# Router logits from the plain residual, filler products on TensorE, pinned places for scatter, gather and transposes, and expert products in steps of four

## The chip, the core and the metric

The kernel runs on one core of a Trainium2 chip. The metric is the device time of one launch in microseconds (us); the profile is one execution of it taken apart by the hardware profiler. Five engines matter: TensorE (PE in the profile; PEld is its weight load), VectorE (DVE), ScalarE (ACT), GpSimd (POOL) and SyncE (SP), which issues nearly all transfers.

## The reference, cut to what matters

Two layers of a hybrid backbone over 256 latent and 256 context tokens of width 1024. The change lies in the second layer's feed-forward part, a mixture of eight SwiGLU experts of which each latent token takes two:

```python
x = x + mod_x[2] * (y_x @ w_out[i])
...
x = x + mod_x[5] * ffn(_modulate(_rms(x, norm2_w[i]), mod_x[3], mod_x[4]))
...
def _modulate(h, shift, scale):
    return h * (1.0 + scale) + shift
...
def _moe(h, router, wg, wu, wd):
    logits = (h @ router).astype(jnp.float32)
    top_v, top_i = lax.top_k(logits, TOP_K)
    gates = jax.nn.softmax(top_v, axis=-1)
    y = jnp.zeros_like(h)
    for e in range(N_EXPERTS):
        w_e = jnp.sum(jnp.where(top_i == e, gates, 0.0), axis=-1).astype(h.dtype)
        y = y + w_e[..., None] * _swiglu(h, wg[e], wu[e], wd[e])
    return y
```

An expert is 1024 x 3584 for gate and up and 3584 x 1024 for down, in float32. A final RMSNorm follows.

## The kernel before

Everything up to the second layer's attention is as in any transformer kernel and isn't touched. What is touched begins with the output projection `project(1, CTX, acc)` (L965), a generator that yields after each step: eight steps for its first three output tiles together, then one for each of five more. Each output tile is added to the residual `x[k]` (128 features x 512 tokens) by DVE at L789, and its square is added to `acc` (L251 to L255).

**Router, L998 to L1071.** PE sums the squares (L288), DVE makes the reciprocal root with twelve small instructions (L266 to L271, L290), and PE spreads it over all partitions (L297, `rbc`). Then eight steps follow: DVE scales `x[k]` (L1013), ACT adds the shift and gives the modulated `hf[k]` (L1014), PE multiplies with the router (L1016, `lg`). The residual is transposed into `xt` beside this (L1006), the modulated tokens into `ht` (L1028). ACT copies the logits (L1018), PE transposes them (L1021), DVE picks the two best experts (L1037 to L1056), PE counts ranks (L1058 to L1062, `rk`), and DVE gets each token's slot in its expert (`pos`) and the counts.

**prepare, L1079.** For an expert, DVE builds a one-hot matrix `oh` of tokens against 96 slots (L1083); PE gathers with it the modulated tokens from `ht` (L1090, `ga`, 16 products, 32 records); ACT copies them into `G` (L1093); PE transposes `oh` (L1096) for the way back.

**experts, L1128.** Eight blocks, one per expert, in an order by how full they are. The 96 slots are three groups of 32. Groups 0 and 1 are always computed; group 2 only when the expert has more than 64 tokens, by an `If` on a PE register (L1136). In a block there are four `up` passes (two halves of the width, gate and up; eight weight tiles each) and one `down` pass (14 tiles). A step of either takes two weight tiles through groups 0, 2, 1, so a block has 16 + 7 such `If`s; the first of each pass has an `Else` that writes zeros. Four products of one tile and group run side by side in four column strips of PE (L1152, L1177); each is two records. Between the passes PE transposes the hidden values (`turn`, L1197), and after `down` `scatter` (L1102) adds up the strips on ACT and DVE (L1107 to L1114) and returns a generator whose eight products (L1121, L1122) add the result to `xt`. In the text these are written behind the next block's gate pass, but the order on each engine is made by a planner that moves an instruction ahead of others when it holds it to be ready.

**Weights.** `Ahead` (L928) streams 46 tiles per block (32 of 896 KB, 14 of 1 MB) from SP into a ring of 16 buffers: tile j+16 is issued when the last product on tile j is done (`load.done`). The first 16 are issued before the router. The numbers of the later experts are read by SP, and all eight group flags by PE, from what the router computed (L1303 to L1305), ahead of the first product.

## Time and profile before

| | us |
|---|---|
| median of three runs | 1833.72 (1830.26 to 1839.75) |
| the profiled execution | 1831.45 |
| its span, first to last instruction | 1829.7 |
| PE / DVE / ACT / POOL busy | 1730.8 / 587.1 / 445.1 / 22.5 |
| read from HBM | 469.36 MB |

The span is read in stages. Up to about 895 us come the first layer and the second layer's attention and projection; from 895 to 924 us the router; from 924 to 1805 us the eight expert blocks; then 25 us of the last scatter, the norm and the store. An engine's busy time says little of whether it bounds; the rows that end its waits do.

### The profile page before, as it was taken

How to read it: one execution, taken by the hardware profiler on the slowest of the kernel's cores; microseconds unless marked ns; L12 is line 12 of the kernel's file. 1: busy time of each engine (PE TensorE's matmuls, PEld its weight loads, DVE VectorE, ACT ScalarE, POOL GpSimd, SP SyncE). 2: the span in 40 equal slices, each digit the busy share in tenths (PEclk: the TensorE clock that was granted, in tenths of full speed). 3: DMA queues.
4: the chain of work that ended last, by engine and by line, in shares of the span. 5: the costliest groups of instructions: out<-in, count | busy, mean ns of one | idle time of the engine just before them, and what ended most of it. 6: DMA issues, size and time to landing. Idle time of an engine off the chain costs nothing. (4 is left out here: it accounts for less than half of the span.)

```text
span 1829.7 us, 31142 instructions
## 1 busy us (share of the span) xinstructions
PE 1730.8 (95%) x13016; PEld 980.7 (54%) x13016; DVE 587.1 (32%) x1356; ACT 445.1 (24%) x852; POOL 22.5 (1%) x47
## 2 busy tenths in 40 slices
PE   6999999999999999999889999999999999999995
PEld 4866458888888898765733333332333323333231
DVE  6635565633333348465410200201011020200213
ACT  4543553432222225544301000100010000100001
POOL 1001000000000000000000000000000000000000
PEclk9999999999999999999989999999999999999997
DMA  7435541332323224454869999898999989999892
GB/s 313 150 119 184 182 161 58 98 98 93 103 92 101 95 81 127 149 195 153 345 243 419 418 419 395 336 389 322 395 418 418 414 335 409 418 418 406 335 419 110
DMA packets 84861, 472.70 MB, mean 258 GB/s; under 512 B 9424, under 2 KB 9808, under 8 KB 69088
## 3 DMA queue, kind: packets, MB, share of 16 engines
q1 hardware_dynamic: 84240, 469.36, 67.4%
q8 instruction: 118, 1.93, 0.4%
q0 software_dynamic: 176, 0.56, 0.1%
q10 hardware_dynamic: 288, 0.52, 0.1%
q14 instruction: 39, 0.32, 0.0%
HBM read 469.36 MB, written 1.05 MB: 257 GB/s over the span
## 5 line engine op out<-in xcount | busy, mean ns | idle before, releaser
L1152 PE MATMUL up<-rawe,G 128*32 128x448 f32 x5120 | 517.7, 551 | 14.0 <-PEq L1136 8.9
L1152 PEld LDWEIGHTS up<-rawe,G 128*32 128x32 f32 x5120 | 168.6, 111 | 337.0 <-issue 309.6
L331 PE MATMUL mm<-hh,wh 128*128 128x512 f32 (+1 forms) x856 | 305.5, 360 | 4.3 <-ACT hh L326 4.2
L332 PE MATMUL mm<-hl,wh 128*128 128x512 f32 (+1 forms) x856 | 304.5, 356 | 0.0
L333 PE MATMUL mm<-hh,wl 128*128 128x512 f32 (+1 forms) x856 | 303.4, 355 | 0.0
L1177 PE MATMUL y<-rawe,e 128*32 128x512 f32 x2240 | 251.2, 594 | 4.0 <-PEq L1136 3.2
L145 ACT ACTIVATE wh<-raw 128x1024 fp32r<-128x1024 f32 x120 | 127.3, 1061 | 326.3 <-PE mm L332 291.2
L146 DVE TENSOR_TENSOR wl<-raw,wh 128x1024 fp32r<-128x1024 f32 x120 | 146.7, 1224 | 174.0 <-ACT wh L145 171.5
L331 PEld LDWEIGHTS mm<-hh,wh 128*128 128x128 f32 x856 | 161.0, 189 | 31.4 <-ACT hh L326 5.5
L332 PEld LDWEIGHTS mm<-hl,wh 128*128 128x128 f32 x856 | 161.8, 189 | 27.3 <-issue 5.2
L333 PEld LDWEIGHTS mm<-hh,wl 128*128 128x128 f32 x856 | 161.7, 189 | 23.5 <-issue 1.6
L1217 DVE TENSOR_TENSOR hid<-sg,up 128x448 f32<-128x448 f32 x48 | 27.1, 617 | 422.8 <-PE up L1152 422.8
L1177 PEld LDWEIGHTS y<-rawe,e 128*32 128x32 f32 x2240 | 73.4, 109 | 158.8 <-issue 151.0
L1109 DVE TENSOR_TENSOR ye<-y,yc 32x512 f32<-32x512 f32 x48 | 32.7, 682 | 200.0 <-ACT yc L1107 199.3
L1198 ACT ACTIVATE e<-hT 128x384 f32<-128x384 f32 x48 | 23.6, 492 | 283.7 <-PE hT L1197 283.1
L1213 ACT ACTIVATE sg<-up 128x448 f32<-128x448 f32 x48 | 22.8, 546 | 218.4 <-PE up L1152 218.4
L331 PE MATMUL mm<-fh,wh 128*128 128x512 f32 (+1 forms) x209 | 74.5, 356 | 0.0
L332 PE MATMUL mm<-fl,wh 128*128 128x512 f32 (+1 forms) x209 | 74.3, 355 | 0.0
L333 PE MATMUL mm<-fh,wl 128*128 128x512 f32 (+1 forms) x209 | 74.3, 355 | 0.0
L210 PE MATMUL ada<-araw,cz 128*32 128x256 f32 x640 | 54.3, 390 | 11.5 <-DMA araw<-in_ada_dram 11.0
L1107 ACT ACTIVATE yc<-y 64x512 f32<-64x512 f32 x24 | 14.3, 596 | 205.0 <-PE y L1177 199.8
L333 PEld LDWEIGHTS mm<-fh,wl 128*128 128x128 f32 x209 | 39.5, 189 | 5.6
(280 smaller groups left out, 1370.8 us busy)
## 6 DMA issues: line engine op xcount, KB each, us to landing
rawe<-in_mg_dram SPq DMA_DIRECT2D x128, 896.0 KB, 10.1
rawe<-in_mu_dram SPq DMA_DIRECT2D x128, 896.0 KB, 11.5
rawe<-in_md_dram SPq DMA_DIRECT2D x112, 1024.0 KB, 14.7
raw<-in_ws_dram SPq DMA_DIRECT2D x120, 512.0 KB, 3.6
araw<-in_ada_dram SPq DMA_DIRECT2D x80, 512.0 KB, 4.4
a<-in_ada_dram SPq DMA_DIRECT2D x8, 1024.0 KB, 11.7
xall<-in_xT_dram SPq DMA_DIRECT2D x2, 1024.0 KB, 6.6
fn<-in_fn_dram POOLq DMA_DIRECT2D x1, 512.0 KB, 5.9
```

Of the source, the lines that this page charges most:

```text
L145: act.activation(h, raw, AF.Copy)
L146: dve.tensor_sub(l, raw, h)
L210: pe.matmul(o[32 * g:32 * g + 32, 0:256], cz[:, kt, 16 - 2 * row:48 - 2 * row], t[:, z:z + 256], start=(first and kt < 4), stop=(last and ...
L331: pe.matmul(out, wh, hh, start=first, stop=False)
L332: pe.matmul(out, wh, hl, start=False, stop=False)
L333: pe.matmul(out, wl, hh, start=False, stop=last)
L1109: dve.tensor_add(ye[32 * s:32 * s + 32, n * 512:(n + 1) * 512], y[s][32 * n:32 * n + 32, :], yc[32 * n:32 * n + 32, :])
L1152: pe.matmul(o[s][32 * c:32 * c + 32, 0:SC], g[:, k, 32 * s:32 * s + 32], w[k][:, c * SC:(c + 1) * SC], start=(k == 0), stop=(k == KT - 1), ...
L1177: pe.matmul(y[s][r:r + 32, :], e[s][:, 2 * i + par, :], w[i - lo][:, par * 1024 + n * 512:par * 1024 + (n + 1) * 512], start=(i == 0), sto ...
L1198: act.activation(e[s][:, 12 * st:12 * st + 12, :], pt[:, 0:384].rearrange("p (q c) -> p q c", c=32), AF.Copy)
L1213: act.activation(sg[s], o[:, 0:SC], AF.Silu)
L1217: dve.tensor_mul(hid[st, s], sg[s], o[:, 0:SC])
```

## The change

The router multiplies the plain residual: the modulation's scale is multiplied into the router's weights ahead of time (`wr`), the shift gives a constant `lc`, and the reciprocal root (`rms`) is multiplied into the transposed logits. Four of the eight logit products are written into the projection. `ht` now holds the plain residual, so one set of transposes is gone; `xt` is copied from it. The gather's one-hot carries `rms`, and scale and shift are applied as `G` leaves PSUM, in eight instructions on ACT and DVE instead of two on ACT. After the transposes PE runs 16 products with zeros, after the ranks 4. `tc.issue_after(ins)` keeps the instructions of its block behind `ins` on the engine of `ins`: the scatter, the gather with the next flag's load, and both transposes of a block are tied so to the last group-1 product of a named step. Steps of `up` take four tiles, of `down` 4, 2, 4 and 4. PE's flags are read one per block instead of all at the start. The zero fills of `yh`, `yl` and `oht` move from GpSimd to ACT.

```diff
+WARM = (16, 4)
+UPS, DOWNS = (0, 4, 8), (0, 4, 6, 10, 14)
...
-    step(p, HEAD)
     wr0 = P1.tile([128, KT, NE], F32, name="wr0")
     nc.gpsimd.dma_start(wr0, a["router"])
+    step(p, HEAD)
...
+    scale, shift = (RW.tile([128, KT], F32, name=n) for n in ("scale", "shift"))
+    dve.scalar_tensor_tensor(scale, mod(1, 4, 0), 1.0, n2[:, 1, :], op0=ALU.add, op1=ALU.mult)
+    dve.tensor_copy(shift, mod(1, 3, 0))
-    nc.gpsimd.tensor_copy(wr[:, :, 0:NE], wr0)
-    A = coef(1, 1)
+    dve.tensor_mul(wr[:, :, 0:NE], wr0, scale.unsqueeze(2).to_broadcast([128, KT, NE]))
+    o = ps("ax", name="lc")
+    for k in range(KT):
+        pe.matmul(o[:, 0:NE], shift[:, k:k + 1].to_broadcast([128, 128]), wr0[:, k, :], start=(k == 0), stop=(k == KT - 1))
+    lc = RW.tile([128, NE], F32, name="lc")
+    act.activation(lc, o[:, 0:NE], AF.Copy)
+    def logits(ks):
+        for k in ks:
+            g = 32 * (k % 4)
+            last = pe.matmul(lg[g:g + 32, 0:256], wr[:, k, :], x[k][:, 256:], start=(k < 4), stop=(k >= 4),
+                             tile_position=(0, g))
+        return last.ins
+    step(p, KT - HEAD + 2)
+    lg = ps("mm", name="lg")
+    logits(range(4))
     run(p)
...
-    S = Stats(acc[0])
-    S.sums(CTX, TOK)
-    for t in range(2):
-        for c in range(2):
-            s = slice(c * 512, (c + 1) * 512)
-            p = ps("ax", name="xT")
-            for q in range(4):
-                pe.transpose(p[:, q * 128:(q + 1) * 128], x[4 * c + q][:, 256 + t * 128:384 + t * 128], ident)
-            act.activation(xt[:, t, s], p, AF.Copy)
-    b = S.spread(CTX, TOK)
-    lg = ps("mm", name="lg")
-    for k in range(KT):
-        u = P1.tile([128, 256], F32, tag="u", name="u", bufs=UB)
-        dve.scalar_tensor_tensor(u, x[k][:, 256:], A[:, k, 0:1], b[:, 256:], op0=ALU.mult, op1=ALU.mult)
-        act.activation(hf[k], u, AF.Identity, bias=mod(1, 3, 0)[:, k:k + 1])
-        g = 32 * (k % 4)
-        pe.matmul(lg[g:g + 32, 0:256], wr[:, k, :], hf[k], start=(k < 4), stop=(k >= 4), tile_position=(0, g))
+    behind_lg = logits(range(4, KT))
     lgs = P1.tile([128, 256], F32, tag="u", name="lgs", bufs=UB)
-    behind_lg = act.activation(lgs, lg[:, 0:256], AF.Copy).ins
-    lg = ps("mm", name="lgT")
-    for t in range(2):
-        pe.transpose(lg[:, t * 128:(t + 1) * 128], lgs[:, t * 128:(t + 1) * 128], ident)
+    act.activation(lgs, lg[:, 0:256], AF.Copy)
+    rms = RS.tile([128, 2], F32, name="rms")
+    with tc.issue_after(behind_lg):
+        o = ps("ax", name="ss")
+        for t in range(2):
+            pe.matmul(o[:, t:t + 1], acc[0][:, CTX + t * 128:CTX + (t + 1) * 128], ones, start=True, stop=True)
+        v = P1.tile([128, 4], F32, tag="v4", name="v4", bufs=2)
+        dve.tensor_scalar(v[:, 0:2], o[:, 0:2], 1.0 / D, EPS, op0=ALU.mult, op1=ALU.add)
+        rsqrt(P1, v[:, 0:2], rms, "n2")
+        lg = ps("mm", name="lgT")
+        for t in range(2):
+            behind_lg = pe.transpose(lg[:, t * 128:(t + 1) * 128], lgs[:, t * 128:(t + 1) * 128], ident).ins
+    def idle(n):
+        o = ps("mm", name="idle")
+        for _ in range(n):
+            pe.matmul(o, zb[:, 0:128], zb, start=True, stop=True)
...
     with tc.issue_after(behind_lg):
         for t in range(2):
             for c in range(2):
-                p = ps("ax", name="tT")
+                s = slice(c * 512, (c + 1) * 512)
+                p = ps("ax", name="xT")
                 for q in range(4):
-                    pe.transpose(p[:, q * 128:(q + 1) * 128], hf[4 * c + q][:, t * 128:(t + 1) * 128], ident)
-                s = slice(c * 512, (c + 1) * 512)
+                    pe_last = pe.transpose(p[:, q * 128:(q + 1) * 128], x[4 * c + q][:, 256 + t * 128:384 + t * 128], ident)
                 behind_th = act.activation(ht[:, t, s], p, AF.Copy).ins
+                last = pe_last.ins
+        with tc.issue_after(last):
+            idle(WARM[0])
...
+    dve.tensor_mul(l0, l0, bc(rms))
+    dve.tensor_add(l0, l0, lc.unsqueeze(1).to_broadcast([128, 2, NE]))
...
-    pe.matmul(rk[:, 2 * NE:3 * NE], onesb, selb[:, 1, :], start=False, stop=True)
+    with tc.issue_after(pe.matmul(rk[:, 2 * NE:3 * NE], onesb, selb[:, 1, :], start=False, stop=True).ins):
+        idle(WARM[1])
...
-        oh = XP.tile([128, 2, SLOTS], F32, tag="oh", name="oh", bufs=1)
+        oh, ohr = (XP.tile([128, 2, SLOTS], F32, tag=n, name=n, bufs=1) for n in ("oh", "ohr"))
         for t in range(2):
-            behind_oh[0] = dve.tensor_scalar(oh[:, t, :], iota[:, 0:SLOTS], poscol(t), None, op0=ALU.is_equal).ins
+            behind_oh[0] = dve.tensor_scalar(ohr[:, t, :], iota[:, 0:SLOTS], poscol(t), rms[:, t:t + 1],
+                                             op0=ALU.is_equal, op1=ALU.mult).ins
         g = XP.tile([128, KT, SLOTS], F32, tag="G", name="G", bufs=2)
         for n in range(2):
             p = ps("ax", name="ga")
             for q in range(4):
                 k = 4 * n + q
                 for t in range(2):
-                    pe.matmul(p[:, q * SLOTS:(q + 1) * SLOTS], ht[:, t, k * 128:(k + 1) * 128], oh[:, t, :],
+                    pe.matmul(p[:, q * SLOTS:(q + 1) * SLOTS], ht[:, t, k * 128:(k + 1) * 128], ohr[:, t, :],
                               start=(t == 0), stop=(t == 1))
-            pv = p[:, 0:4 * SLOTS].rearrange("p (q c) -> p q c", q=4)
-            act.activation(g[:, 4 * n:4 * n + 4, :], pv, AF.Copy)
+            for q in range(4):
+                k, z = 4 * n + q, p[:, q * SLOTS:(q + 1) * SLOTS]
+                if q % 2:
+                    dve.tensor_scalar(g[:, k, :], z, scale[:, k:k + 1], shift[:, k:k + 1], op0=ALU.mult, op1=ALU.add)
+                else:
+                    act.activation(g[:, k, :], z, AF.Identity, scale=scale[:, k:k + 1], bias=shift[:, k:k + 1])
+        for t in range(2):
+            dve.tensor_scalar(oh[:, t, :], iota[:, 0:SLOTS], poscol(t), None, op0=ALU.is_equal)
         p = ps("ax", name="ohT")
         for t in range(2):
             pe.transpose(p[0:SLOTS, t * 128:(t + 1) * 128], oh[:, t, :], ident)
...
                 else:
-                    body(s)
+                    behind[0] = body(s).ins
...
-            for k0 in range(0, KT, 2):
+            for k0, k1 in zip(UPS, UPS[1:]):
                 def body(s):
-                    for k in (k0, k0 + 1):
+                    for k in range(k0, k1):
...
                         if s == GROUPS[-1]:
                             load.done(KT - 1 - k)
+                    return last
...
                 groups(b, body, zero, k0 == 0)
+                if k1 == KT:
+                    for s in GROUPS:
+                        consume(s, o[s])
                 yield
-            for s in GROUPS:
-                consume(s, o[s])
...
-        def down(b, y, e, lo, hi):
-            w = load.take(hi - lo)
-            for i0 in range(lo, hi, 2):
+        def down(b, y, e):
+            w = {}
+            for i0, i1 in zip(DOWNS, DOWNS[1:]):
+                for i, t in enumerate(load.take(i1 - i0)):
+                    w[i0 + i] = t
...
-                    for i in (i0, i0 + 1):
+                    for i in range(i0, i1):
...
                         if s == GROUPS[-1]:
-                            load.done(hi - 1 - i)
+                            load.done(i1 - 1 - i)
+                    return last
...
                 u = up(b, g, st, gate)
-                step(u, 2)
+                step(u)
                 if st:
-                    turn([hid[0, i] for i in range(3)], e, 0)
+                    with tc.issue_after(behind[0]):
+                        turn([hid[0, i] for i in range(3)], e, 0)
                 run(u)
                 u = up(b, g, st, product)
-                if not st and pending:
+                for _ in range(2):
+                    if not st and pending:
+                        with tc.issue_after(behind[0]):
+                            step(pending)
                     step(u)
-                    step(pending)
-                    step(u)
-                    step(pending)
                 run(u)
             y = [ps("y", name="y") for _ in range(3)]
-            u = down(b, y, e, 0, 6)
-            step(u, 2)
-            turn([hid[1, i] for i in range(3)], e, 1)
-            run(u)
-            u = down(b, y, e, 6, 14)
+            u = down(b, y, e)
+            step(u)
+            with tc.issue_after(behind[0]):
+                turn([hid[1, i] for i in range(3)], e, 1)
             step(u, 2)
             if b + 1 < len(blocks):
-                nxt = prepare(blocks[b + 1][0])
+                with tc.issue_after(behind[0]):
+                    nxt = prepare(blocks[b + 1][0])
+                    if flags:
+                        flags.append(flag(b + 1))
             run(u)
             pending = scatter(y, oht, blocks[b][1])
         run(pending)
...
     for z in (yh, yl, *(o.rearrange("p t c -> p (t c)") for o in ohts)):
-        nc.gpsimd.tensor_copy(z[SLOTS:128, :], zb[SLOTS:128, 0:1].to_broadcast([128 - SLOTS, z.shape[1]]))
+        with tc.issue_after(behind_th):
+            act.activation(z[SLOTS:128, :], zb[SLOTS:128, 0:1].to_broadcast([128 - SLOTS, z.shape[1]]), AF.Copy)
+    with tc.issue_after(behind_th):
+        for t in range(2):
+            act.activation(xt[:, t, :], ht[:, t, :], AF.Copy)
...
-    flags = [nc.values_load(f[0:1, p:p + 1], engines=(mybir.EngineType.PE,), min_val=0, max_val=1)
-             for p, f in enumerate([third0] + [third] * (NE - 1))]
-    experts(blocks, loader, first, flags)
+    def flag(p):
+        return nc.values_load((third if p else third0)[0:1, p:p + 1], engines=(mybir.EngineType.PE,), min_val=0, max_val=1)
+    experts(blocks, loader, first, flag)
```

## Rows read from the trace of the kernel before

**Rows 1.** Windows: stretch, length, busy (count) PE/PEld/DVE/ACT/POOL, PEclk, DMA share, GB/s.

```profile
924.20:1019.20 95.00, 89.61 (x810) 34.02 (x814) 5.93 (x15) 8.11 (x15) 0.00 (x0) 0.96 0.92 376
...
1019.20:1143.30 124.10, 121.66 (x1174) 42.90 (x1170) 15.23 (x27) 9.64 (x19) 0.00 (x0) 0.99 1.01 410
...
1489.40:1587.10 97.70, 90.95 (x826) 32.83 (x822) 15.19 (x27) 9.58 (x19) 0.00 (x0) 0.97 0.96 387
...
1711.20:1804.80 93.60, 86.83 (x792) 29.36 (x788) 14.42 (x24) 8.64 (x17) 0.00 (x0) 0.96 0.83 334
```

**Rows 2.** Waits, experts' stretch: who waited for whom, total us, times, longest.

```profile
PE up L1152 <- PEq L1136: 8.9, 38, 1.1
...
PE up L1152 <- DMA rawe<-in_md_dram: 0.2, 1, 0.2
```

**Rows 3.** Timeline of SP: start, us, queue, line, transfer, count.

```profile
878.17 20.67 SPq L943 DMA_DIRECT2D rawe<-in_mu_dram  x8
...
932.15 10.27 SPq L943 DMA_DIRECT2D rawe<-in_mg_dram  x8
```

**Rows 4.** Windows of 40 us within the first block.

```profile
960.00:1000.00 40.00, 38.76 (x364) 16.56 (x359) 4.16 (x12) 5.41 (x11) 0.00 (x0) 1.00 1.01 419
```

**Rows 5.** Timeline, PE in the router: start, us, instruction, count [idle <-releaser].

```profile
897.03 0.58 PE L288 MATMUL ss<-ones,acc 128*128 128x1 f32 x4 [1.64 <-DVE acc L255]
...
902.45 0.62 PE L1016 MATMUL lg<-xall,wr 128*32 128x256 f32 x2 [1.12 <-ACT xall L1014]
...
909.75 0.44 PE L1021 MATMUL lgT<-sml,lgs 128*128 128x128 f32 x2
...
913.21 0.17 PE L1058 MATMUL rk<-selb,ltri 128*128 128x8 bf16 x1 [3.01 <-DVE selb L1056]
...
914.21 5.90 PE L1090 MATMUL ga<-oh,ht 128*128 128x96 f32 x32 [0.73 <-DVE oh L1083]
...
924.21 0.95 PE L1152 MATMUL up<-rawe,G 128*32 128x448 f32 x1 [3.88 <-issue]
```

**Rows 6.** Timeline of DVE in the router.

```profile
897.64 0.16 DVE L290 TENSOR_SCALAR v<-ss 128x2 f32<-128x2 f32 x1 [0.76 <-PE ss L288]
...
899.81 0.16 DVE L271 SCALAR_TENSOR_TENSOR r<-rst,rsy 128x2 f32<-128x2 f32 x1
...
910.23 0.23 DVE L1037 TENSOR_REDUCE l<-lgT 128x16 f32<-128x64 f32 x1 [5.64 <-PE lgT L1021]
...
913.80 0.45 DVE L1083 TENSOR_SCALAR oh<-sml,pos 128x96 f32<-128x96 f32 x2
```

**Rows 7.** The instructions of line 1305: duration ns min/median/max, first and last start.

```profile
L1305 PEldq TENSOR_LOAD <-third x8: 297/302/492, 918.5 to 923.5; - x8
```

**Rows 8.** Timeline of PE around two scatters, one gather.

```profile
1496.57 1.22 PE L1121 MATMUL scat<-yh,oht 128*128 128x512 f32 x2 [3.22 <-ACT yh L1113]
...
1557.75 2.59 PE L1090 MATMUL ga<-oh,ht 128*128 128x96 f32 x22
...
1594.30 1.07 PE L1121 MATMUL scat<-yh,oht 128*128 128x512 f32 x2 [1.89 <-ACT yh L1113]
```

**Rows 9.** Windows: the granted clock in four stretches.

```profile
897.50:900.30 2.80, 2.80 (x18) 2.78 (x19) 1.95 (x12) 1.79 (x3) 0.00 (x0) 0.62 1.01 415
...
927.40:932.00 4.60, 4.60 (x28) 1.50 (x32) 0.00 (x0) 0.00 (x0) 0.00 (x0) 0.50 0.02 4
...
1496.60:1502.00 5.40, 5.40 (x20) 1.56 (x20) 1.47 (x2) 0.00 (x0) 0.00 (x0) 0.50 0.42 175
...
1594.30:1598.00 3.70, 3.70 (x18) 0.93 (x18) 1.20 (x1) 0.00 (x0) 0.00 (x0) 0.54 1.02 422
```

**Rows 10.** Timeline of PE: products of a two-group step, and of three-group steps.

```profile
1517.00 3.21 PE L1152 MATMUL up<-rawe,G 128*32 128x448 f32 x32 [0.18 <-PEq L1136]
...
1633.19 35.66 PE L1152 MATMUL up<-rawe,G 128*32 128x448 f32 x376
```

**Rows 11.** Groups of instructions by line: count, busy us, mean ns, idle before.

```profile
L1113 ACT ACTIVATE yh<-ye 96x1024 fp32r<-96x1024 f32 x8 | 8.5, 1057 | 27.2 <-DVE ye L1112 27.2
```

More of the change, by code (lines that the diff above doesn't have):

```diff
@@ L1126, in scatter, with experts @@
         return add()
-    def experts(blocks, load, first, flags=None):
+    def experts(blocks, load, first, flag=None):
+        behind, flags = [None], [flag(0)] if flag else None
         def groups(b, body, zero, first):
@@ L1176, in body @@
                                 r = 32 * (2 * par + n)
-                                pe.matmul(y[s][r:r + 32, :], e[s][:, 2 * i + par, :],
-                                          w[i - lo][:, par * 1024 + n * 512:par * 1024 + (n + 1) * 512],
-                                          start=(i == 0), stop=(i == 13), tile_position=(0, r), skip_group_check=True)
+                                last = pe.matmul(y[s][r:r + 32, :], e[s][:, 2 * i + par, :],
+                                                 w[i][:, par * 1024 + n * 512:par * 1024 + (n + 1) * 512],
+                                                 start=(i == 0), stop=(i == 13), tile_position=(0, r),
+                                                 skip_group_check=True)
                         if s == GROUPS[-1]:
-                            load.done(hi - 1 - i)
+                            load.done(i1 - 1 - i)
+                    return last
                 def zero(s):
```

11 lines of the change are left out of this document (5 added, 6 removed).

## The prediction

> **What bounds the kernel now.** I read the windows by block first, then the waits of PE, then the timelines of the places where PE stood still. The eight expert blocks take 880.6 us of the span. They come in two lengths: four with three groups take 124.1 us each (one stands in the rows, the other three have the same length), three with two groups 97.9, 97.7 and 93.6, and the first, also of two groups, 95.0 [rows 1]. In a block PE is busy for 91 to 98% of the time, and among its waits one of 0.2 us is put down to a weight transfer [rows 2]. So PE, not DMA, sets the pace of the blocks, though DMA runs at 410 GB/s beside it [rows 1] and at 419 where PE holds nothing back [rows 4]. The reader is to see that both are nearly full: a block is 32 tiles of 896 KB and 14 of 1 MB, 44.04 MB, which is 105.1 us at 419 GB/s, and PE needs 110 us on average.
>
> Two stretches are not like that. In the router all engines work in a chain of short steps: from the last projection product, which ends 1.64 us before the sum of squares at 897.03, so at 895.4, to the first expert product at 924.21 are 28.8 us [rows 5]. SP issues its last early tile before 899 and the next one at 932.15 [rows 3], when the first product has freed a buffer. And at each block's start PE waits for the scatter: 1.89 us ahead of a three-group block, 3.22 ahead of a two-group one [rows 8].
>
> **The router, from the last product.** Now: 1.64 us of residual, square and sum, then PE's `ss`, twelve small DVE instructions from 897.64 to 899.97 [rows 6], the spread, eight modulation steps with their products from 902.45 to the logits' transposes at 909.75 [rows 5], the choice from 910.23 to the ranks at 913.21, the one-hot at 913.80 [rows 6], the gather's 5.90 us at 914.21, and 3.88 us in which PE does nothing ahead of 924.21 [rows 5].
>
> After: the spread and the eight steps are gone, the reciprocal root stays. Counted from the last product's end, the root is ready at 4.6 (899.97 - 895.39). The logits' copy and transposes need about 2.5 and lie beside it. The choice starts with a multiply and an add more, 0.2 each like DVE's other small steps [rows 6]; with the reduction, 5.2. The choice takes what it took from its second step, 913.21 - 910.49 = 2.7, so the ranks could run at 7.9.
>
> Here the change adds something in the way. PE has 16 transposes from about 2.4 (2.8 us now [rows 9]) and behind them 16 products with zeros of 512 columns; `rk` is queued behind these, and all of DVE waits for `rk`. Two scatter products of 512 columns took 1.07 at half clock [rows 8], so such a product takes some 0.25 at full and 0.5 at half clock: the sixteen take 4 to 8 us and end between 9.2 and 13.2. While PE was full of transposes the clock fell to 0.62 on average [rows 9], so it may well be low as they begin. The Trainium skill ("TensorE: Matmul & The Clock Gate", Part 4, PE-mode transpose) says that transposes don't count as work for the clock, and that row agrees; by it the ranks would wait for the late end. I take 10, thus 2 us of delay.
>
> From the ranks to the one-hot took 1.0 [rows 5], so the gather starts at 11. It took 5.90 with the clock falling and rising; 22 of the same records take 2.59 at full clock [rows 8], so 32 take 3.8. I take that, since products run until just before. Then eight short instructions on two engines instead of one of ACT, about 0.6. The 3.88 us of idleness are PE reading eight flags: the reads start at 918.5 and the last at 923.5, 0.71 apart [rows 7]. One read stays, and lies beside the gather. Its seven sisters move into the `down` passes: between nothing (PE's queue is full there) and 0.7 each, 5 us; I take nothing, as a whole step of products is queued ahead. The ACT fills and copies that come from GpSimd and from the second transposes are four instructions of 1024 and two of 256 elements a row, 1.06 for a long one [rows 11], about 5 us on ACT between the last transposes and the first gather; they end near 11, so they delay `G` by 0 to 1. New work inside the projection, eight narrow products and four logits at 0.62 a pair [rows 5], costs 0.5 to 1.5, say 1.2.
>
> Sum: 11 + 3.8 + 0.6 + 1.2 = 16.6 instead of 28.8, a gain of 12. Bounds: 15 if the filler never delays, 6 if it runs at half clock throughout and the gather too.
>
> **The blocks.** (a) Scatter. Its source is ready 7.2 us after the block starts (1594.30, when ACT's `yh` released it, against 1587.1), but the planner put it behind one or two products. Tied behind the gate pass, it has 16 tile-group products at 0.76 ahead of it (eight records of 35.66 / 376 = 0.095 [rows 10]), 12.1 us, or 18.2 with three groups; the wait goes. With it goes the low clock behind the wait: 5.4 us at 0.50 in a two-group block, 3.7 at 0.54 in a three-group one [rows 9], worth 2.7 and 1.7. So 3.6 for four blocks and 5.9 for three: 32 us. What is late next there is nothing up to 12 us.
>
> (b) Steps of four. Where group 2 is skipped, a step of 32 records begins 0.17 late and its own end isn't covered by the next: 3.21 + 0.17 = 3.38 against 32 x 0.095 = 3.03 [rows 10], 0.35 per skip. Per block 23 tests become 12, 11 fewer, in four blocks: 15.4 us. The waits agree in kind, 8.9 us over 38 in the up passes [rows 2]. Three-group blocks show no such gap.
>
> (c) The first block runs at half clock (0.50, 1.2 GHz) for 4.6 us and in the 3.2 before it [rows 9], of which PE is busy for 6.7: with a clock kept up, 3.3 us.
>
> (d) Gather and transposes behind named steps: the gather's 32 records are as many as before and have the last step of `down` behind them, at least eight tile-group products, 6.9 us, in which `G` is evacuated. A tied transpose that waits for the two PSUM buffers costs 0.4 as now. I take zero, bounds -3 to +8 (1.2 per block if PE must wait for the second one-hot).
>
> Sum of (a) to (c): 51 us. The last 25 us stay.
>
> **Does DMA allow it?** The first buffer comes free after 4 x 0.76 + 0.2 + 0.76 = 4 us of the first block, at 912 + 4 = 916 instead of 932. From there 352.3 MB less 14.7 take 806 us at 419 GB/s: 1722 at the earliest. PE would end its last block at 1804.8 - 12 - 51 = 1742. How far DMA is ahead, block by block: after the first (95.0 - 3.3 - 3.9 = 88 us of PE, to 1000; the next block's first tile is 30 tiles or 70 us on, 986) 14 us; each three-group block adds 120.5 - 105.1 = 15; each two-group block (88) takes 17, the last (84) 21. So 14, 29, 44 but no more than the ring of about 35, then 18, 33, 16, 31, 10. It stays positive, but landing and the four tiles that are held until a step's end take some of it, so that after the fifth and in the last block PE may wait. I charge 3 us, bounds 0 and 8.
>
> Forecast: 12 + 51 - 3 = 60 less. The sum is made against the profiled execution, 1831.45 us, 2.3 below the median of the three runs: 1771 us.
>
> **Rivals.**
> 1. DMA becomes the bound: at the 410 GB/s of the three-group blocks [rows 1] the same bytes take 824 us from 916, with 9 of pause at the full ring, the last step's 4 and landing 4: 1757 instead of 1745, so 1783. For it: DMA has been full in those blocks; against it: 419 where PE frees buffers in time.
> 2. The scatter's wait only moves (to the two PSUM buffers that DVE must empty, or to the next step's place): half of its 32 us stay, 1787. Against it: the products ahead of it last twice as long as its source needs.
> 3. The router gains 5 rather than 12, by the filler at half clock: 1778.
> 4. The order doesn't obey, for example since the planner already had such an order for other reasons: without (a) 1803.
> 5. Slower: a skip jumps over 64 records' worth of instructions instead of 32. If the target has not been fetched, PE waits for its code. In the first block such waits reach 1.1 us, later ones 0.2 [rows 2]. 28 skips without zeros remain; the gain of 60 is lost when each costs 2.1 us more, and at 3 us the time would be 1855. The Trainium skill ("Runtime: NRT & Kernel Launch", Instruction fetch mechanics) says a taken branch outside the window of fetched code stalls for a fetch; the 38 short waits here show that nearly all targets were inside it.
>
> **How the numbers follow.** Chances: the forecast 0.49, rival 1 0.13, rival 2 0.14, rival 3 0.11, rival 4 0.06, slower by rival 5 0.04, no visible change, from rival 5 near its point, 0.03. The forecast's own range, from its bounds, is 1757 to 1784. The low end takes the bounds of the router, of (d) and of DMA, 9 together, and 5 for the first block's waits for code going too; the high end the router's 6, (d)'s 8 and the rest of DMA's, which do not all come together. To hold 8 in 10 it goes on past rival 2 to 1797; rivals 4, 5 and no change, 0.13, stay out. Faster by over 0.5%, which is about what a measurement of this kernel tells from no change: 0.93; within it 0.03; slower 0.04.
>
> **What would show it.** The first expert product 15 to 18 us after the last projection product, at 910 to 914; SP's next tile at 916; PE at full clock at the first block. Blocks of 119 to 121 and 86 to 89 us; no wait for `yh` ahead of a scatter; seven gaps by PE's sequencer in a two-group block. The first waits of PE for `rawe` late in a two-group block. I'd be wrong if blocks don't shorten where group 2 runs (scatter), if `rk` starts later than 11 us after the last product (filler), or if DMA stays under 410 GB/s while PE waits for it.

## The result and the profile after

| | before | after |
|---|---|---|
| median, us | 1832.97 (1830.26 to 1839.75) | 1776.47 (1773.89 to 1778.33) |
| ratio after / before | | 0.9685, 95% interval 0.9656 to 0.9715 |
| profiled execution | 1831.45 | 1775.88 |
| its span | 1829.7 | 1774.1 |

The change gives 56.5 us, against 60 forecast from the profiled execution; 1776.5 stands 5.5 above the 1771 predicted and inside the range.

First the windows of four blocks of the changed kernel, as [rows 1] has them of before (stretch, length, busy PE / PEld / DVE / ACT / POOL, granted clock, DMA share, GB/s): the first block, a three-group one, a two-group one, the last.

```profile
912.40:999.20 86.80, 85.59 (x813) 35.52 (x816) 11.19 (x38) 9.77 (x20) 0.00 (x0) 1.00 1.00 412
999.20:1120.90 121.70, 121.64 (x1176) 45.43 (x1172) 17.18 (x33) 10.27 (x21) 0.00 (x0) 1.00 1.01 418
1242.50:1331.70 89.20, 87.82 (x824) 34.37 (x820) 17.18 (x33) 10.24 (x20) 0.00 (x0) 1.00 1.01 418
1664.20:1749.20 85.00, 83.10 (x790) 31.89 (x786) 14.42 (x24) 8.51 (x16) 0.00 (x0) 1.00 0.95 393
```

In a block PE is now busy for 98 to 100% of the time, at a clock of 1.00 (2.4 GHz) throughout, where [rows 1] showed 93 to 98% (the prediction read 91). The reader should look at the last column too: the weights now come at 418 GB/s, and no window of 100 us of any kernel here shows more than 419. The four three-group blocks take 121.7 each, the two-group ones 86.8, 89.2, 89.2 and 85.0. Against 95.0, 97.9, 97.7 and 93.6 and 4 x 124.1 that is 43.6 us less.

PE's waits in the experts' stretch (who for whom, total us, times, longest), to set beside [rows 2]:

```profile
PE up L1185 <- PEq L1169: 2.6, 13, 0.3
PE y L1215 <- PEq L1169: 1.2, 7, 0.2
PE up L1185 <- DMA rawe<-in_mu_dram: 0.6, 2, 0.4
PE y L1215 <- SPq L1360: 0.5, 1, 0.5
PE up L1185 <- DMA rawe<-in_mg_dram: 0.2, 1, 0.2
```

The waits of a scatter for `yh` [rows 8] are gone altogether, the sequencer's in the up passes fell from 8.9 us over 38 to 2.6 over 13, and weights cost PE 0.8; 0.5 more, in the last block, is put down to SP's own queue.

The router, PE's timeline, beside [rows 5]:

```profile
899.35 0.28 PE L337 MATMUL mm<-hh,wl 128*128 128x256 f32 x1
...
901.30 0.44 PE L1032 MATMUL lgT<-sml,lgs 128*128 128x128 f32 x2 [0.47 <-ACT lgs L1021]
...
901.94 1.95 PE L1046 MATMUL xT<-sml,xall 128*128 128x128 f32 x16
903.73 3.62 PE L1037 MATMUL idle<-zb 128*128 128x512 bf16 x16
907.62 0.17 PE L1081 MATMUL rk<-selb,ltri 128*128 128x8 bf16 x1 [0.28 <-DVE selb L1079]
...
908.68 3.80 PE L1115 MATMUL ga<-ohr,ht 128*128 128x96 f32 x32
912.41 1.31 PE L1185 MATMUL up<-rawe,G 128*32 128x448 f32 x9
```

From the last projection product's end (899.63) to the first expert product are 12.8 us; before they were 28.8. The zero products end at 907.35, and the ranks wait 0.28 for DVE's choice, not for PE. SP's next tile follows the first freed buffer at 918.23 instead of 932.15 [rows 3], 5.8 us after the first expert product where the prediction had 4:

```profile
879.82 23.34 SPq L947 DMA_DIRECT2D rawe<-in_mu_dram  x8
918.23 8.80 SPq L947 DMA_DIRECT2D rawe<-in_mg_dram  x8
```

The 55.5 us by which the last block ends earlier in the trace (1749.22 instead of 1804.77) are therefore 16.0 in the router and 43.6 in the blocks, less 2.5 that the projection is longer, and less 1.7 by which this execution was already late before the projection's changed part. Executions drift that early, whatever the kernel: the logits' transposes (`lgT`) start between 898.2 and 905.8 us in kernels whose code is the same up to there. Where traces are compared below I count from `lgT` to the end of the last block (the first ACT copy of its scatter), 847.92 us in the changed kernel.

### The profile page after: what moved, and what is told of

Same layout as the page of the kernel before. It is cut to its first block, busy times and chain, and to the rows that moved or that the text cites. A ratio compares the mean times of both kernels' runs of the same rounds, so it can differ in the third digit from the quotient of the medians.

```text
span 1774.1 us, 31022 instructions
## 1 busy us (share of the span) xinstructions
PE 1713.3 (97%) x13032; PEld 997.4 (56%) x13032; DVE 600.1 (34%) x1400; ACT 448.6 (25%) x863; POOL 19.4 (1%) x42
## 5 line engine op out<-in xcount | busy, mean ns | idle before, releaser
L1185 PE MATMUL up<-rawe,G 128*32 128x448 f32 x5120 | 507.2, 540 | 3.7 <-PEq L1169 2.6
L1185 PEld LDWEIGHTS up<-rawe,G 128*32 128x32 f32 x5120 | 184.3, 110 | 301.0 <-issue 280.4
L1215 PE MATMUL y<-rawe,e 128*32 128x512 f32 x2240 | 263.7, 593 | 1.8 <-PEq L1169 1.2
L1215 PEld LDWEIGHTS y<-rawe,e 128*32 128x32 f32 x2240 | 78.3, 110 | 160.9 <-issue 155.4
L1239 DVE COPY e<-hT 64x128 f32<-64x128 f32 x48 | 13.6, 284 | 163.3 <-ACT e L1238 163.2
L1154 DVE SCALAR_TENSOR_TENSOR xt<-scat,wet,xt 128x512 f32<-128x512 f32 x32 | 22.6, 746 | 117.4 <-PE scat L1153 117.3
## 6 DMA issues: line engine op xcount, KB each, us to landing
rawe<-in_mg_dram SPq DMA_DIRECT2D x128, 896.0 KB, 17.4
rawe<-in_md_dram SPq DMA_DIRECT2D x112, 1024.0 KB, 19.1
```

The lines of the kernel that those rows point to most:

```text
L1185: last = pe.matmul(o[s][32 * c:32 * c + 32, 0:SC], g[:, k, 32 * s:32 * s + 32], w[k][:, c * SC:(c + 1) * SC], start=(k == 0), stop=(k == K ...
L1215: last = pe.matmul(y[s][r:r + 32, :], e[s][:, 2 * i + par, :], w[i][:, par * 1024 + n * 512:par * 1024 + (n + 1) * 512], start=(i == 0), s ...
```

## The experiments

All are compared with the kernel before on the same chip, whose median in those sets was 1829 to 1832 us. Four kernels take the change apart first.

**1. The scatter's pin alone.** The kernel before, with one edit:

```diff
-                    step(u)
-                    step(pending)
-                    step(u)
-                    step(pending)
+                    for _ in range(2):
+                        with tc.issue_after(behind[0]):
+                            step(pending)
+                        step(u, 2)
```

> The kernel before with one edit: the scatter's two steps are kept behind the gate pass's last group-1 product and behind the second step of the product pass. By the sum: seven boundaries lose PE's wait for yh (four of 1.89, three of 3.22 us) and the low clock after it (1.7 and 2.7 us), 32 us, so about 1801 us; three-group blocks 120.5 us, two-group blocks 91.8, PE at full clock across the boundary. Rival, the wait only moves: a wait ahead of the scatter's products at the new place, and half of the 32 us or less. Rival, the planner's order has little to do with it: within 5 us of the kernel before.

Measured: 1798.97 us against 1830.34, ratio 0.9825 (0.9807 to 0.9842), 31.4 us. In its trace no scatter waits for `yh`; the three-group blocks take 120.1 (4.0 less), the two-group ones 91.8 and 91.7 (6.0 less), the last 87.6. So the price of step (a), 3.6 and 5.9, held as forecast; counted from `lgT`, the trace gives 35.0 us in all.

**2. The changed kernel without that pin.**

```diff
                     if not st and pending:
-                        with tc.issue_after(behind[0]):
-                            step(pending)
+                        step(pending)
```

> The changed kernel with the scatter's pin taken away, all else kept. If the pin carries (a): the waits for yh and the low clock come back, 25 to 32 us more than the changed kernel, 1801 to 1808 us. Rival: the steps of four and the other pins already hold the scatter back, so that it stays within 8 us of the changed kernel.

Measured: 1834.63, ratio 1.0023 (1.0013 to 1.0032). The whole gain is gone, 58 us rather than the 25 to 32 expected. PE's wait, and one of the seven in the timeline with the products behind it:

```profile
PE scat L1152 <- ACT yh L1144: 34.3, 7, 4.9
```

```profile
1003.80 1.22 PE L1152 MATMUL scat<-yh,oht 128*128 128x512 f32 x2 [4.90 <-ACT yh L1144]
1004.95 1.72 PE L1185 MATMUL up<-rawe,G 128*32 128x448 f32 x8
```

In the kernel before the same wait was 1.9 or 3.2 us. Left to the planner, with steps of four, the scatter comes behind 16 records of the block instead of 32 or 48, so each boundary waits 4.9 us, and the products behind the wait run at half clock (eight records in 1.72 us, 0.21 each, against 0.095 [rows 10]). The pin is thus worth 31 us in the old order and 58 in the new one: it also pays for what the longer steps would do to an order left free.

**3. The expert part alone** (the old router, without zero products, with the new steps, pins, and flags in their places; `G` leaves PSUM as in the kernel before; the cut is against the changed kernel):

```diff
-            for q in range(4):
-                k, z = 4 * n + q, p[:, q * SLOTS:(q + 1) * SLOTS]
...
+            pv = p[:, 0:4 * SLOTS].rearrange("p (q c) -> p q c", q=4)
+            act.activation(g[:, 4 * n:4 * n + 4, :], pv, AF.Copy)
```

> The router of the kernel before with the expert part of the changed one (all pins, steps of four, flags read one per block). If the parts add up as in the sum: scatter 32, skips 15, and the 3.9 us in which PE read eight flags, 51 us less the blocks' own 1 us each that the changed kernel showed over the sum, so a gain of 43 to 47 and a time of 1786 to 1790; the first block still starts at half clock. If the router's earlier start is what lets the blocks run (the tiles would come too late or too early otherwise): blocks longer than in the changed kernel by more than 1 us and waits of PE for rawe.

Measured: 1782.01, ratio 0.9734 (0.9714 to 0.9754), 48.3 us less, somewhat more than expected. One part of the text before the run was wrong: the first block doesn't start at half clock. With the seven reads gone PE stands idle nowhere between the gather and the first products, and the windows behind the first product, here and in the kernel before, show clocks of 1.00 and 0.56:

```profile
922.66:932.00 9.34, 9.16 (x95) 3.71 (x98) 0.78 (x3) 0.38 (x1) 0.00 (x0) 1.00 0.33 115
```

```profile
924.20:933.50 9.30, 8.16 (x46) 2.45 (x50) 0.00 (x0) 0.00 (x0) 0.00 (x0) 0.56 0.06 12
```

So this block takes 85.8 us. The other blocks are of 120.6 and 88.2 us (120.9 and 88.5 the last two; the last waits 2.6 us for weights), which the prediction gave for the changed kernel (120.5 and 88) and which the changed kernel misses by 1.1. The difference is told by the gather's end. Here, one ACT copy per half, and the transposes of the one-hot follow the gather at once:

```profile
1653.99 3.81 PE L1091 MATMUL ga<-oh,ht 128*128 128x96 f32 x32
1656.05 0.49 ACT L1094 ACTIVATE G<-ga 128x384 f32<-128x384 f32 x1 [15.33 <-PE ga L1091]
...
1657.64 0.38 PE L1097 MATMUL ohT<-sml,oh 128*96 128x128 f32 x2
```

In the changed kernel, timeline of the same place:

```profile
1650.54 2.73 PE L1115 MATMUL ga<-ohr,ht 128*128 128x96 f32 x23
...
1652.40 0.43 ACT L1122 ACTIVATE G<-ga,shift,scale 128x96 f32<-128x96 f32 x1 [0.45 <-DVE G L1120]
1652.86 0.38 DVE L1120 TENSOR_SCALAR G<-ga,scale,shift 128x96 f32<-128x96 f32 x1 [0.50 <-ACT G L1122]
...
1653.77 0.38 DVE L1120 TENSOR_SCALAR G<-ga,scale,shift 128x96 f32<-128x96 f32 x1 [0.53 <-ACT G L1122]
1654.17 0.18 PEld L1127 LDWEIGHTS ohT<-sml,oh 128*96 128x96 f32 x2 [0.84 <-DVE G L1120]
1654.18 0.43 PE L1127 MATMUL ohT<-sml,oh 128*96 128x128 f32 x2
```

ACT and DVE take turns on one PSUM buffer and never overlap: each waits 0.45 to 0.53 for the other. A half takes 1.7 us instead of 0.49, and PE's transposes start when DVE has done its first turn on the second half, 0.9 us after the four turns of the first half ended at 1653.24. So they wait for the evacuations; why for this one rather than for the first half's last isn't shown. The Trainium skill ("PSUM — Partial Sum Buffer", PSUM bank collisions raise a hardware error) says that two engines may not touch the same bank in the same cycle and that the program has to keep them apart; the turns agree with that, though the trace doesn't tell whether the turns come from the bank or from the common tile `G`.

**4. The router alone** (the new router, with the old steps and no pins, all eight flags read at the start):

```diff
-    experts(blocks, loader, first, flag)
+    flags = [nc.values_load(f[0:1, p:p + 1], engines=(mybir.EngineType.PE,), min_val=0, max_val=1)
+             for p, f in enumerate([third0] + [third] * (NE - 1))]
+    experts(blocks, loader, first, flags)
```

> The router of the changed kernel with the expert part of the one before (steps of two, no pins, eight flags at the start). By the sum the gain is 12 less 3.9 for the flags, less 1.2 for the shift's products in the projection that took 1.7, plus 3.3 for the first block at full clock: 9 to 12 us, about 1821. The first expert product about 16.5 us after the projection's last product. If the filler or the eight short instructions of G cost more in every block: under 5 us.

Measured: 1813.21, ratio 0.9898 (0.9880 to 0.9916), 17.1 us less where 9 to 12 were expected. In its trace the first expert product comes 12.8 us after the last projection product; then PE reads the flags:

```profile
918.58 14.20 PE L1183 MATMUL up<-rawe,G 128*32 128x448 f32 x128 [5.16 <-issue]
```

By the first block's end 16.0 - 2.2 (this block is 97.2 us from its first product, against 95.0) - 2.5 = 11.3 us are won, as expected. The rest, 5.8, of which the trace shows 5.1, comes later: three of its three-group blocks take 122.5 instead of 124.1, and the last block 92.7 instead of 93.6. Its waits for `yh` are the same, 17.2 us in seven, but behind these three the clock doesn't fall. The 5 us behind the wait in the first such block, in the kernel before and here:

```profile
1026.40:1031.40 5.00, 4.92 (x28) 1.51 (x32) 2.24 (x3) 0.00 (x0) 0.00 (x0) 0.66 1.02 420
```

```profile
1015.80:1020.80 5.00, 4.95 (x44) 1.77 (x48) 2.63 (x3) 0.00 (x0) 0.00 (x0) 1.00 1.01 419
```

In the one three-group block that still takes 124.5 us they are at 0.66 again. Why the clock falls behind one wait of 1.9 us and not behind another isn't shown. So these 5 us are part of what the pin gains too, and can't be had twice.

The next four change the new kernel in one place each.

**5 and 6. `G` out of PSUM in fewer turns.** In the first, one DVE multiplication per half, and the shift added from SBUF to SBUF. In the second ACT takes the first half and DVE the second.

```diff
-            for q in range(4):
...
+            gn = g[:, 4 * n:4 * n + 4, :]
+            dve.tensor_mul(gn, p[:, 0:4 * SLOTS].rearrange("p (q c) -> p q c", q=4),
+                           scale[:, 4 * n:4 * n + 4].unsqueeze(2).to_broadcast([128, 4, SLOTS]))
+            dve.tensor_add(gn, gn, shift[:, 4 * n:4 * n + 4].unsqueeze(2).to_broadcast([128, 4, SLOTS]))
```

> The changed kernel, but each half of the gathered rows leaves PSUM in one DVE multiplication over four chunks, and the shift is added from SBUF to SBUF, in place of four short instructions that ACT and DVE take in turn. Theory (PSUM buffer): a block of the changed kernel is 1.1 us over its forecast since the eight turns hold both gather buffers until 3.5 us after the first half, so that the transposes of the one-hot wait; then blocks of three groups come back from 121.7 to 120.6 us and blocks of two from 89.2 to 88.2, and the time falls by 7 boundaries x 1.0 = 7 us, to about 1769. Rival (the block): the 1.1 us lie in the block itself (the flag's read, a skip over longer bodies), and the time stays at 1776.

```diff
-                if q % 2:
+                if n:
```

> The changed kernel, but ACT takes all four chunks of the gather's first half and DVE all four of the second, in place of turns within a half. If two engines cannot read one PSUM bank at once but can read two, the halves overlap: the first is free after 4 x 0.43 = 1.7 us, the second after 4 x 0.38 = 1.5 us, the wait of the transposes goes for the most part, and the time falls by 5 to 7 us to 1769 to 1771. If the turns come from the tile that both write (each instruction waits for the one before it, wherever it reads), DVE starts its half only when ACT has done its own, nothing overlaps, and the time stays within 2 us of 1776.

Measured: 1771.49, ratio 0.9690 (0.9662 to 0.9717), and 1771.51, ratio 0.9691 (0.9662 to 0.9720). Against their own set's 1829.12 neither ratio can be told from the 0.9685 of the changed kernel, so the traces have to decide. Both bring the blocks back as the theory says: 120.6 and 88.0 to 88.2 in the first, 120.8 and 88.3 to 88.7 in the second (but for the last three-group block, 121.2 and 121.3). In the first, the transposes follow the gather:

```profile
1641.51 3.81 PE L1115 MATMUL ga<-ohr,ht 128*128 128x96 f32 x32
1643.57 0.56 DVE L1118 TENSOR_TENSOR G<-ga,scale 128x384 f32<-128x384 f32 x1 [15.01 <-PE ga L1115]
...
1645.15 0.38 PE L1125 MATMUL ohT<-sml,oh 128*96 128x128 f32 x2
```

So the 1.1 us per boundary are the turns. But the last block is 88.5 instead of 85.0, with new waits in it, and with a lower clock behind them (a row of the waits, and a window):

```profile
PE y L1213 <- DMA rawe<-in_md_dram: 2.6, 2, 1.4
```

```profile
1715.00:1720.00 5.00, 3.61 (x24) 0.87 (x28) 0.00 (x0) 0.00 (x0) 0.00 (x0) 0.74 1.01 421
```

From `lgT` to the end the first takes 844.21 us and the second 845.92, 3.7 and 2.0 less than the changed kernel: half of the 7 us is given back to the weights, nearly all of it in the last block. The second kernel doesn't tell why the engines take turns, since DVE's half was gathered only when ACT had done with its own.

**7. Steps of two again,** with the side work pinned behind the same products:

```diff
-UPS, DOWNS = (0, 4, 8), (0, 4, 6, 10, 14)
+UPS, DOWNS = (0, 2, 4, 6, 8), (0, 2, 4, 6, 8, 10, 12, 14)
...
```

> The changed kernel with the weights taken two tiles at a step again (eleven steps in a block in place of six; the order of side work stays bound behind the same products). Theory of the prediction: a block of two groups has five to eleven more skips (the four of up in place of two, the seven of down in place of four: five more) at 0.35 us, so 5 x 0.35 x 4 blocks = 7 us more, and a block of three groups gains nothing, so about 1783; the 11 fewer skips that the prediction counted would give 15 us, so 1791. Rival (the skips are hidden once nothing else waits): under 2 us, 1776 to 1778.

Measured: 1795.13, ratio 0.9811 (0.9782 to 0.9839). That text's own count of five tests is wrong: a block has four up passes, so 23 tests instead of 12, as the prediction had it, and its 1791 is the number to set beside the result. The three-group blocks are the same 121.7, the later two-group ones 4.5, 4.7 and 4.0 longer, and the first 6.0 from `lgT`, 19.1 us in all. One step of 32 records, and its gap:

```profile
1503.60 3.21 PE L1185 MATMUL up<-rawe,G 128*32 128x448 f32 x32 [0.17 <-PEq L1169]
1506.98 2.57 PE L1185 MATMUL up<-rawe,G 128*32 128x448 f32 x24 [0.17 <-PEq L1169]
```

From start to start 3.38 us, the number of [rows 10]. Eleven tests cost 4.0 to 4.7 us in a later block, 0.36 to 0.43 each, against the 0.35 of step (b).

**8. No zero products.**

```diff
-        with tc.issue_after(last):
-            idle(WARM[0])
...
-    with tc.issue_after(pe.matmul(rk[:, 2 * NE:3 * NE], onesb, selb[:, 1, :], start=False, stop=True).ins):
-        idle(WARM[1])
+    pe.matmul(rk[:, 2 * NE:3 * NE], onesb, selb[:, 1, :], start=False, stop=True)
```

> The changed kernel without the 16 and 4 zero products that fill TensorE's waits in the router. Theory (clock): TensorE is idle for 3.7 us before the ranks, so the ranks, the gather (3.8 us for 32 products) and the start of the first block run at the lower clock: 2 to 3 us more in the gather and 3 us more in the first block, in all 4 to 6 us, about 1781. Rival (the filler does nothing, since the wait is too short for the clock to fall, or since it delays the ranks as much as it gives): within 1.5 us of 1776.

Measured: 1780.55, ratio 0.9722 (0.9698 to 0.9747); from `lgT` to the end 853.49 us, 5.6 more. Its timeline, and then its windows for the clock:

```profile
912.13 0.17 PE L1079 MATMUL rk<-selb,ltri 128*128 128x8 bf16 x1 [3.74 <-DVE selb L1077]
...
913.20 6.85 PE L1112 MATMUL ga<-ohr,ht 128*128 128x96 f32 x32 [0.80 <-DVE ohr L1104]
```

```profile
912.00:916.00 4.00, 3.07 (x20) 3.01 (x19) 2.84 (x20) 1.70 (x4) 0.00 (x0) 0.69 1.01 393
916.00:920.00 4.00, 4.00 (x23) 3.83 (x23) 1.33 (x8) 0.95 (x3) 0.00 (x0) 0.50 1.00 396
920.00:924.00 4.00, 4.00 (x21) 1.02 (x24) 1.82 (x10) 2.14 (x3) 0.00 (x0) 0.53 0.68 284
```

Behind 3.7 us without work the granted clock drops to 0.50 (1.2 GHz), the gather takes 6.85 instead of 3.80, and the first block, which starts at 0.53, is 2.2 us longer. The ranks start 6.32 us after `lgT` (905.81 here), exactly as in the changed kernel (901.30 to 907.62): the zero products delay nothing and are worth 5 us in this kernel. Experiment 3 reaches the full clock in the first block without them, but its gather takes 5.41 us.

The last four ask what bounds the kernel now.

**9. All flags at the start.**

```diff
-        behind, flags = [None], [flag(0)] if flag else None
+        behind, flags = [None], [flag(i) for i in range(len(blocks))] if flag else None
...
-                    if flags:
-                        flags.append(flag(b + 1))
```

> The changed kernel, but TensorE reads all eight flags ahead of the first block, as the kernel before did, in place of one ahead of each block. The prediction put the seven later reads at nothing, with 5 us as a bound. If they are hidden behind queued products, the early reads cost seven more loads, 3.7 to 4.5 us ahead of the first block and nothing comes back: 1780. If each later read costs its 0.6 us on TensorE, the sum stays even: 1776.

Measured: 1783.35 where 1780 was expected, ratio 0.9737 (0.9713 to 0.9760); from `lgT` 854.00 us, 6.1 more. All of it lies before the first block's end: PE waits 4.8 us on the reads, and its clock falls (windows):

```profile
916.00:920.00 4.00, 2.14 (x12) 0.61 (x16) 0.00 (x0) 0.00 (x0) 0.00 (x0) 0.72 0.33 135
920.00:924.00 4.00, 4.00 (x40) 1.26 (x36) 0.00 (x0) 0.00 (x0) 0.00 (x0) 0.86 0.00 0
```

The later blocks are equal within 0.03 us (121.67, 121.67, 89.17, 121.69, 89.18, 121.66, 84.96), so a flag read behind a queued step costs nothing.

**10. A ring of 12 buffers.**

```diff
-NRW = (8, 8)
+NRW = (8, 4)
```

> The changed kernel with 12 weight buffers in place of 16. Theory (the stream is at its limit): the four buffers hold 4 x 2.2 us of transfer, so the lead of 10 us that the shortest transfers still had in the changed kernel falls to about nothing in the blocks of two groups, waits for weights appear there, and the stream ends later by the four tiles that were not loaded ahead of the first block: 9 to 15 us more, 1785 to 1791. Rival (the weights are hidden anyway, as they were in the kernel before): within 2 us of 1776.

Measured, one execution: 1800.29; from `lgT` 871.60 us, 23.7 more where 9 to 15 were expected. The three-group blocks keep their 121.7 to 122.0, the first block is 6.9 longer, the later two-group ones become 94.7, 95.1 and 90.1, and PE waits for down weights:

```profile
PE y L1215 <- DMA rawe<-in_md_dram: 14.3, 13, 1.4
```

In the two-group blocks PE uses weights faster than they come and lives off the lead that a three-group block built up, and the ring limits this lead.

**11 and 12. Longer steps,** alone and with edit 5:

```diff
-UPS, DOWNS = (0, 4, 8), (0, 4, 6, 10, 14)
+UPS, DOWNS = (0, 8), (0, 6, 10, 14)
...
```

> The changed kernel with the eight tiles of an up pass in one step and ten tiles of down in three (seven tests of the flag in a block in place of twelve). Theory (skips): with 0.41 us for each test that a block of two groups loses (18 us for 44 tests when the steps were halved), 5 fewer tests in 4 blocks give 8 us: 1768. Rival (the stream of the weights): the changed kernel moves 419 GB/s from 1300 to 1740 us of its trace, so the weights already arrive as fast as they can; what the early blocks of two groups gain is given back as waits for weights in the last ones, and tiles that are held for longer steps start their successors later: within 3 us of 1776, with waits for the weights of several us in the last blocks.

> Both edits at once: the gathered rows leave PSUM in one multiplication per half, and the steps are those of eight tiles. If TensorE's work set the end, the gains add up: 1776 - 5 - 8 = 1763. If the stream of the weights does (the first of the two edits alone already shows 2.6 us of waits for down weights in the last block, where the changed kernel shows none), the second edit adds next to nothing to the 1771 of the first: 1769 to 1773, with more waits for weights.

Measured: 1789.95, ratio 0.9775 (0.9749 to 0.9801), and 1786.56, ratio 0.9753 (0.9728 to 0.9777). Both theories missed, and so did the rival of the first, which had the waits but within 3 us of 1776: fewer tests made it 13 us slower. The side work moves too, since it is pinned behind whole steps. Waits of PE in the first of the two, and then its windows:

```profile
PE y L1215 <- DMA rawe<-in_md_dram: 9.6, 9, 1.4
PE up L1185 <- DMA rawe<-in_mg_dram: 8.6, 6, 2.0
```

```profile
1100.00:1200.00 100.00, 100.00 (x990) 40.08 (x986) 15.82 (x29) 9.02 (x17) 0.00 (x0) 1.00 0.90 363
1300.00:1400.00 100.00, 94.94 (x878) 35.80 (x870) 15.86 (x30) 9.95 (x19) 0.00 (x0) 0.98 1.01 419
```

The transfers pause while PE is full (363 GB/s) and PE waits while the transfers run at 419. A tile is handed back when the last group passes over it. With eight tiles in a step, half of the ring is held until then, the stream stops, and the lead is gone when a two-group block's down pass and the gate pass behind it need it. The changed kernel had 401 GB/s in the first of these windows. From `lgT` this kernel takes 17.6 us more; waits for weights make 18.9 (9.6, 8.6 and 0.7), so the moved side work isn't needed to explain it. Steps of four lie between two costs: tests on one side, held buffers on the other.

## Why the prediction was right, and by how much it was off

It was right within 5.5 us. In the profiled execution the last block ends at 1749.2 instead of the 1745 forecast, and its steps are off in both directions, so part of the closeness is luck: the router's surplus and an unspent charge for DMA offset a cost that the forecast had at zero. Two of its signs were missed, 12.8 us where it had 15 to 18, and blocks of 121.7 where it had 119 to 121.

- **Router.** Forecast 16.6 from the last product, of which 1.2 for the projection; measured 12.8 and 2.5. The step that failed is the filler's delay, taken as 2 us: it is 0. The 0.6 for the eight evacuations falls away too, since the first product starts at 912.41, as the gather ends (908.68 + 3.80). The sixteen zero products took 3.62 us, below the 4 to 8 worked out, since the clock had not fallen ahead of them. The transposes of which [rows 9] showed 0.62 followed a pause; here they follow the dense projection and ran at 1.00 (16 in 1.95 us). The Trainium skill's sentence on transposes ("TensorE: Matmul & The Clock Gate", Part 4, PE-mode transpose), by which the late end would have come, didn't decide it: the transposes kept the clock that the work before them had left. Whether the pause or the transposes lowered it in [rows 9] isn't shown. The projection's term was mis-sized: the eight products for `lc` alone are sixteen records and take 1.85 us, and the last product comes 23.3 us after the `g2p` products instead of 20.75, in every kernel with the new router.
- **(a) Scatter, 32 us.** Right: 31.4 alone (35.0 by the trace), no wait for `yh` left, three-group blocks 4.0 and two-group ones 6.0 shorter (forecast 3.6 and 5.9).
- **(b) Steps of four, 15.4 us.** Right in kind, a little small: 17.4 by the last blocks' ends in experiment 7, 19.1 counted from `lgT`.
- **(c) The first block's clock, 3.3.** Right in kind: 1.00 from the first product on; without the zero products the first block loses 2.2 us and the gather 3.1. But the zero products aren't the only way to it: in experiment 3 the clock is 1.00 there as soon as the flags' reads are gone.
- **(d) Gather and transposes pinned, 0, bounds -3 to +8.** This is the step that failed. The prediction named a wait for the second one-hot, 1.2 per block, and left the wait of the transposes for a PSUM buffer at 0.4 as before; what came is a wait of PE's transposes for the evacuations, because the eight short ones take turns. It costs 1.1 in each of seven boundaries, 7 to 8 us, as experiments 3, 5 and 6 show. The prediction had priced these eight instructions at 0.6 in the router, as eight durations that overlap on two engines, and had not carried them to the other seven boundaries.
- **DMA, 3 us, bounds 0 to 8.** In the changed kernel the weights cost PE 0.8. The lead account was right that it stays positive, but only just: as soon as the 7 us of (d) go, 4 come back as waits for weights and the lower clock behind them. A three-group and a two-group block together take 121.7 + 89.2 = 210.9 us, and their 88.1 MB at 419 GB/s take 210.2. The change ended where rival 1 begins.
- **The flags' later reads, 0, bounds 0 to 5.** Right (experiment 9).

Against the forecast's 1745 that makes: this execution's late start +1.7, projection +1.3, router -2.6; blocks 836.8 against 830 and 3 for DMA, +3.8; together 4.2, which is the whole difference at the last block's end.

The rivals: rival 1 did not happen, since the stream ran at 418 rather than 410. Rival 2 fell with experiment 1, and its idea, a wait that moves, is true of the kernel without the pin only. Rival 3 fell with the 12.8 us, rival 4 with experiment 2: the order obeys, and without it there would be nothing. Rival 5 fell: of the twenty waits for the sequencer (13 and 7) none is longer than 0.3 us. The Trainium skill ("Runtime: NRT & Kernel Launch", Instruction fetch mechanics) tells of taken branches that stall for a fetch; whether any of these twenty is such a stall, the trace doesn't tell.

One sign was only half right: the forecast's parts add up (12 + 51 - 3), but the parts measured alone, 17.1 and 48.3, sum to 65.4, and together they give 56.5. By the traces, stage by stage, 10.4 are missing. Of these 5.1 are the low clock behind the scatter's wait, which in experiment 4 mostly stays away by itself and with the pin goes in any case, so that the sum counts it twice. In the seven later blocks 2.3 more are missing: the turns cost 5.9 there, and 3.6 of them come back because the last block of experiment 3 waits for weights and the changed kernel's hardly does. The other 3.0 lie ahead of the first block's end; the turns are 0.9 of them, and the rest I haven't taken apart.

No version here is shown to beat the changed kernel. The nearest is experiment 5 by its trace, 3.7 us; its measured ratio is the same.

## What to carry to other kernels

Pin side work behind a named product when its source needs a known time; here the pin alone gave 31 us, and the changed kernel without it gained nothing. When a bound moves close to a second one, add up what a pair of unequal blocks needs of each resource: the next few microseconds on PE were half given back to a weight stream that was already at its rate, and a longer step made it worse by holding buffers. Price an evacuation that is split over two engines by the time that its turns take from first to last, not by the engines' busy time.

## What was not expected of the hardware

- ACT and DVE on one PSUM buffer and one tile came strictly in turns in this program, each released by the other: 0.43 and 0.38 us of work, each with 0.45 to 0.53 of waiting for the other. In experiment 6 the same four instructions on ACT alone took 1.40 in a row, on DVE alone 1.24.
- Sixteen transposes behind a dense stretch ran at a granted clock of 1.00, and 3.7 us without work right behind them brought it to 0.50; 4.8 us on flag reads brought it to 0.72 and 0.86 in the windows behind. The same wait of 1.9 us ahead of a scatter was followed by 0.66 over 5 us in the kernel before and by 1.00 in three blocks of experiment 4.
- The weights' stream has a flat ceiling here: 418 to 419 GB/s in the windows of 100 us in which buffers came free in time, with 12 buffers or 16.
